# Gates and branches as [token, channel], with operand octets on multiples of 64 bytes

## The chip, the core and the metric

One core of a Trainium2 chip runs the whole program. Its engines work side by side and wait for each other through semaphores: TensorE (PE; its weight loads are shown apart as PEld), VectorE (DVE), ScalarE (ACT), GpSimd (POOL) and SyncE (SP), which here issues the loads. The metric is the device time of one execution in microseconds (us); lower is better.

## What is computed

Two decoder blocks over 256 tokens of 2048 channels, in float32. The change lies in the first block's mixer. Three branches (a gated delta rule, sliding-window attention, stick-breaking attention) give `y_dn` (1024 channels), `y_swa` and `y_sb` (512 each). Each is projected to 2048 channels, multiplied by a gate of its own, and the sum goes through one more projection:

```python
proj = xn @ w_in                       # gates: its last 3 * 2048 columns
gate = jax.nn.sigmoid(gates).reshape(bsz, seq, N_BRANCH, D_MODEL)
merged = gate[:, :, 0] * (y_dn @ w_br_dn) + gate[:, :, 1] * (y_swa @ w_br_swa) \
       + gate[:, :, 2] * (y_sb @ w_br_sb)
return merged @ w_o
```

`xn` is the RMS-normalized input. The rest (cross attention to `mem`, a gated MLP with a short convolution, and a second block with an HGRN recurrence, a pooling mixer and a squared-ReLU MLP) is as usual, and of it only the matmuls matter here.

## The kernel before

**Numbers.** A float32 matrix product is made of float32r products: each operand is split in a high part and a remainder, and three products are added (high x high, high x remainder, remainder x high). Weights come in *chunks* of 8 blocks of 128x128 (512 KB); SP loads two chunks at a time into `wr` (three such buffers). ACT writes a chunk's high part `wh` (`split_hi`, L264), DVE the remainder `wl` in two halves of 128x512 (`split_lo`, L273), two chunks ahead of their use. The program uses 854 chunks, and TensorE is meant to work on them without a pause.

**Operands.** Activations stand as [channel, token] in *octets*: tiles `[128, 8, 2, 256]` of float32r, 16 KB in each partition, that hold high part and remainder of 8 blocks of 128 channels. Two octets make an `Operand`. `P0` (P0a, P0b) and `P1` (P1a, P1b) live for the whole program, behind the tile of small vectors `vec`, which has 481 columns. In the built program they start at bytes 20512, 36896, 53280 and 69664 of each partition, all 32 past a multiple of 64. The octets P2a, P2b, P2c and YH, which some stages add, start on multiples of 64, and so do `wr`, `wh` and `wl`.

**Two forms of a product.** `gemm` calls `mm` (L283 to L291) for each block: the weights are stationary, and the octet's block moves, first high part and remainder together (512 columns, L290), then the high part again under the weights' remainder (256 columns, L291). The result is [channel, token], one block of 128 channels a bank, in two halves that `evac` (from L379) adds: ACT copies one, DVE adds the other and multiplies by the token's norm. `gemm_nat` (from L359) turns the roles: a block of the octet for 128 tokens is stationary, and 512 columns of weights move, in three matmuls (L373 high x high, L374 remainder x high, L375 high x remainder). The result is [token, channel], 512 channels in two banks, one for each half of the tokens. A chunk is 8 pairs in the first form and 12 matmuls in the second.

**Order.** All instructions are written out by one Python program in a fixed order. Beside the stream of matmuls run generators ("tasks") that emit their next instructions at a *slot*; there is one slot after each block of a chunk. `until` runs slots without matmuls until something holds.

**Around the change.** For each of 16 blocks of 128 channels, `gates(d)` makes three gates from `Ax` (the normalized input, in P0): 6 chunks, evacuated, multiplied by the norm, sigmoid. `branches(d, ...)` makes the three products from `Ay` (P1): 2 chunks, evacuated; POOL multiplies each by its gate and adds the three into `M[:, d]`. When the last `gates` is through, `merged_gen` splits the 16 blocks of `M` into `Am` (P0 again), from which the output projection `w_o` reads; it starts with two blocks of output side by side (`gemm_first`), so that the last 4 of the 16 input blocks are needed only after 24 pairs. During the 16 steps SP also loads `mem` and `x`, and ACT and POOL add up the squares of `mem` (`Sm`), whose column sums (L429) TensorE makes in the projection.

The second form is used before by five places: stick-breaking values (P0), cross-attention values (P0), values and gates of the second block (P1), and the last MLP's output (P0b, P2a, P2b, P2c in turn).

Of the kernel before, what the change touches and what calls it, by code (L numbers as in the profile page):

```python
# [9 lines left out]
F32 = mybir.dt.float32  # L10
# [3 lines left out]
AF = mybir.ActivationFunctionType  # L14
# [13 lines left out]
def _consts():  # L28
# [37 lines left out]
    ("ffn_conv", 192), ("norm_final", 16), ("norm_mix_pre_2", 16), ("norm_mix_post_2", 16),  # L66
    ("norm_mlp_pre_2", 16), ("pool_b_2", 8), ("pool_scale_2", 8),
    ("lb_logits_2", 16), ("hgrn_norm_w_2", 8), ("dn_norm", 1), ("dn_a_log", 8),
    ("dn_dt_bias", 8), ("swa_sinks", 8),
]  # L70
_VOFF = {}
_n = 0
for _k, _w in _VECS:
    _VOFF[_k] = (_n, _w)
    _n += _w
_VN = _n
FIRST = {"w_swa": 4, "w_o": 2, "w_mi": 4}


# [6 lines left out]
def tile_kernel(ctx, tc, a, out, dbg=None):  # L86
# [120 lines left out]
    plan("w_dn", 0, 64)  # L207
    plan("w_sbv", 0, 8)
    plan("w_sbqk", 0, 16)
    for d in range(16):  # L210
        plan("w_gate", 6 * d, 6)
        plan("w_br", 2 * d, 2)
    plan("w_o", 0, 32)
    plan("w_xq", 0, 8)
    plan("w_xk", 0, 8)
# [140 lines left out]
            if k == 15:  # L356
                then(t, ps[t])

    def gemm_nat(A):  # L359

        ps = []
        for c in range(8):
            w = Chunk()
            hv = w.h.rearrange("p (k n) c -> p k (n c)", k=2)
            lv = w.l.rearrange("p (k n) c -> p k (n c)", k=2)
            for t in range(2):
                if c == 0:
                    ps.append(bank("pn"))
                for k in range(2):
                    kk = 2 * c + k  # L370
                    wait_for(A, kk)
                    s, e = (c == 0 and k == 0), (c == 7 and k == 1)
                    PE.matmul(ps[t], A[kk][:, 0, cs(t)], hv[:, k], start=s, stop=False)  # L373
                    PE.matmul(ps[t], A[kk][:, 1, cs(t)], hv[:, k], start=False, stop=False)  # L374
                    PE.matmul(ps[t], A[kk][:, 0, cs(t)], lv[:, k], start=False, stop=e)  # L375
                    w.block(2)
        return ps
# [712 lines left out]
    def gate_gen(o, p):  # L1090
        yield from evac(o, p, Nx)
        act(o, o, AF.Sigmoid)
        yield 2
# [7 lines left out]
    def branch_gen(d, m, b, p, gate):
        o = M[:, d] if b == 0 else m[:, b - 1]
        yield from evac(o, p)
        G.tensor_tensor(o, o, gate, op=ALU.mult)
        if b == 2:
            yield 4
            G.tensor_tensor(m[:, 0], m[:, 0], m[:, 1], op=ALU.add)
            G.tensor_tensor(M[:, d], M[:, d], m[:, 0], op=ALU.add)
            yield 6
            merged[0] += 1  # L1110

    def branches(d, g3):
        m = mp.tile([128, 2, T], F32, name="m", tag="m", bufs=2)
        for b, (n0, n1) in enumerate(((0, 8), (8, 12), (12, 16))):
            p = bank()
            if b != 2:
                w = Chunk()
            for k in range(n0, n1):
                mm(p, w.h[:, k % 8], w.l[:, k % 8], Ay[k], k == n0, k == n1 - 1)
                w.block()  # L1120
            spawn(branch_gen(d, m, b, p, g3[:, b]))

    gp = gates(0)
# [5 lines left out]
    MT = mc.enter_context(tc.tile_pool(name="mt", bufs=1)).tile([128, 16, T], F32, name="MT")  # L1129
    mc2 = ExitStack()  # L1130
    mp = mc2.enter_context(tc.tile_pool(name="mm", bufs=1))
    M = mp.tile([128, 16, T], F32, name="M")
    Sm = Squares()
    Am = Operand(*P0)

    def merged_gen():
        for n in range(16):
            while merged[0] <= n:
                yield 1
            yield from split(Am, n, M[:, n])  # L1140

    for d in range(16):
        if d:
            gp = gates(d)
        if d == 15:
            spawn(merged_gen())
        branches(d, gp)
        if d < 8:
            s4 = slice(4 * (d % 4), 4 * (d % 4) + 4)
            nc.sync.dma_start(MT[:, s4] if d < 4 else X[:, s4], (a["mem"] if d < 4 else a["x"])[:, s4])  # L1150
        else:
            spawn(Sm.add(MT[:, 2 * d - 16]))
            spawn(Sm.add(MT[:, 2 * d - 15]), 4)

    def residual(n, p, gain, A, *sums):

# [532 lines left out]
            V.scalar_tensor_tensor(y, t, 1.5, y, op0=ALU.add, op1=ALU.mult)  # L1689
            return y  # L1690

    eps = cp.tile([128, 1], F32, name="eps")
    G.memset(eps, EPS)
    post5 = Post()
    S5 = post5.Sq
    gain5 = W("norm_mix_post_2")
# [55 lines left out]
    nat = {}  # L1752
    ss7 = ec.tile([128, 2, 4], F32, name="ss7")
    pre7 = ec.tile([128, 2], F32, name="pre7")

    def ch(g):
        return slice(512 * g, 512 * g + 512)

    def flip_x_gen():
        while not all(A2_.ok):  # L1760
# [151 lines left out]
def layout(i):  # L1912
    i = {k: np.asarray(v) for k, v in i.items()}
    cat = np.concatenate
    x = _feat(i["x"][0])
    o = {"x": x, "xg": cat([_vec(i["norm_mix"][0]), x[:, 0:2].reshape(128, -1)], 1), "mem": _feat(i["mem"][0]), "cst0": _CARR[0], "cst1": _CARR[1], "cst2": _CARR[2]}
    w = i["w_in"][0]
    qkv, z, ab, sq, skv, sb, gt = np.split(
        w, np.cumsum([3072, 1024, 16, 512, 256, 1536]), axis=1)
    grp = []  # L1920
    for g in range(4):
        s = slice(256 * g, 256 * g + 256)
        grp += [qkv[:, 1024:2048][:, s], qkv[:, 0:1024][:, s], qkv[:, 2048:][:, s], z[:, s]]
    o["w_dn"] = _tiles(cat(grp, 1))
    o["w_ab"] = ab.reshape(16, 128, 16).transpose(1, 0, 2).reshape(128, 256)
    sq = sq.reshape(D, 2, 4, 64).transpose(0, 2, 1, 3).reshape(D, 512)
    o["w_swa"] = _tiles(cat([skv, sq], 1))
    o["w_sbqk"] = _tiles(sb[:, 0:1024].reshape(D, 2, 4, 128).transpose(0, 2, 1, 3).reshape(D, 1024))
    o["w_sbv"] = _rows(sb[:, 1024:])
    o["w_gate"] = _tiles(gt.reshape(D, 3, 16, 128).transpose(0, 2, 1, 3).reshape(D, 6144))  # L1930
    swa = i["w_br_swa"][0].reshape(2, 4, 64, D).transpose(1, 0, 2, 3).reshape(512, D)
    o["w_br"] = _tiles(cat([i["w_br_dn"][0], swa, i["w_br_sb"][0]], 0))
# [40 lines left out]
    o["vec"] = cat([v[n] for n, _ in _VECS], 1)  # L1973
# [22 lines left out]
```

## Time and profile before

| | us |
|---|---|
| median of 3 runs (2615.05 to 2616.28) | 2615.83 |
| the profiled execution | 2615.93 |
| its span, first to last instruction | 2613.9 |
| TensorE busy in the span | 2572.2 |
| DVE busy | 1872.2 |
| ACT busy | 1363.3 |
| POOL busy | 341.0 |

The granted TensorE clock is 0.997 of full speed over the span. A matmul's row gives its start and how long it takes from start to end; since matmuls are pipelined, the next one starts earlier than that, and the distance of two starts is what it costs in a stream. In the rows by time the columns are start, duration, engine, line, operation, written tile <- read tiles, stationary and moving sizes; in brackets stands idle time ahead of it and what ended it.

### The profile page before, as it was taken

The page shows a single profiled execution, that of the slowest core. Times are in us where ns is not written, and L with a number is a line of the kernel's source. Part 1 is how long each engine was busy: PE and PEld are TensorE (multiplying, and loading weights), DVE is VectorE, ACT ScalarE, POOL GpSimd, SP SyncE. Part 2 cuts the span into 40 slices and gives each one's busy share as a digit, 9 for nine tenths or more (in the row PEclk, how much of TensorE's full clock was granted, in tenths as well). Part 3 has the DMA queues.
Part 4 walks back from the last instruction along what each step waited for, and adds up shares of the span by engine and source line. Part 5 has one row for each costly group of instructions (what it writes and reads, how often), then busy time and mean ns, then how long its engine had stood idle before and what let it go on. Part 6 is the DMA issues. An engine that isn't in the chain of part 4 may idle for free.

```text
span 2613.9 us, 39511 instructions
## 1 busy us (share of the span) xinstructions
PE 2572.2 (98%) x15277; PEld 2196.4 (84%) x15277; DVE 1872.2 (72%) x3487; ACT 1363.3 (52%) x2157; POOL 341.0 (13%) x326
## 2 busy tenths in 40 slices
PE   8999999999999999999999999999899999999998
PEld 7888888888888888888888888878788888888886
DVE  7787766667777788888866687976675575665665
ACT  6655545555555565555544454555564444443443
POOL 1122111222321010000001102721010000000000
PEclk9999999999999999999999999999999999999999
DMA  6433435555555445555555554345445555555553
GB/s 226 137 138 130 146 130 194 212 207 185 186 179 192 163 160 194 187 184 193 180 191 182 194 178 161 114 145 193 145 171 188 189 190 197 181 190 193 201 190 141
DMA packets 66428, 461.17 MB, mean 176 GB/s; under 512 B 7360, under 2 KB 7616, under 8 KB 11840
## 3 DMA queue, kind: packets, MB, share of 16 engines
q1 hardware_dynamic: 65952, 457.86, 50.2%
q8 instruction: 120, 1.97, 0.3%
q10 hardware_dynamic: 288, 0.79, 0.1%
q14 instruction: 68, 0.56, 0.1%
HBM read 456.52 MB, written 2.10 MB: 175 GB/s over the span
## 4 chain that ended last, share of the span: by engine, by line
PE 86%; DVE 8%; ACT 3%; issue 3%; POOL 0%; DVEq 0%; ACTq 0%; POOLq 0%
PE pg L290 40%; PE pg L291 20%; PE pn L373 6%; PE pn L374 6%; PE pn L375 6%; PE pg L288 3%; DVE wl L273 3%; PE pg L287 1%; ACT wh L264 1%; PE ph L1459 0%; PE pz L754 0%; DVE QK L987 0%; DVE Wt L1431 0%; DVE P0b L416 0%; DVE P1b L418 0%
## 5 line engine op out<-in xcount | busy, mean ns | idle before, releaser
L273 DVE TENSOR_TENSOR wl<-wr,wh 128x512 fp32r<-128x512 f32 x1708 | 1218.8, 749 | 308.6 <-ACT wh L264 307.6
L264 ACT ACTIVATE wh<-wr 128x1024 fp32r<-128x1024 f32 x854 | 902.9, 1058 | 860.8 <-PE pg L288 331.7
L290 PE MATMUL pg<-P1a,wh 128*128 128x512 f32 x1360 | 492.2, 400 | 4.6 <-DVE P1a L418 4.6
L290 PE MATMUL pg<-P1b,wh 128*128 128x512 f32 x1188 | 430.7, 399 | 1.4 <-ACT wh L264 1.4
L290 PE MATMUL pg<-P0a,wh 128*128 128x512 f32 x1040 | 383.0, 404 | 6.9 <-ACT wh L264 6.9
L291 PE MATMUL pg<-P1a,wl 128*128 128x256 f32 x1360 | 383.5, 282 | 3.3 <-DVE wl L273 3.3
L290 PE MATMUL pg<-P0b,wh 128*128 128x512 f32 x1031 | 378.6, 403 | 0.3 <-DVE P0b L416 0.3
L291 PE MATMUL pg<-P1b,wl 128*128 128x256 f32 x1188 | 334.7, 282 | 2.9 <-DVE wl L273 2.8
L290 PEld LDWEIGHTS pg<-P1a,wh 128*128 128x128 f32 x1360 | 257.0, 189 | 59.0 <-issue 5.0
L291 PE MATMUL pg<-P0a,wl 128*128 128x256 f32 x1040 | 292.9, 282 | 0.0
L291 PE MATMUL pg<-P0b,wl 128*128 128x256 f32 x1031 | 289.9, 281 | 1.1 <-DVE wl L273 1.1
L291 PEld LDWEIGHTS pg<-P1a,wl 128*128 128x128 f32 x1360 | 258.4, 190 | 13.6 <-DVE wl L273 6.1
L290 PEld LDWEIGHTS pg<-P1b,wh 128*128 128x128 f32 x1188 | 223.3, 188 | 53.9 <-ACT wh L264 2.0
L290 PEld LDWEIGHTS pg<-P0a,wh 128*128 128x128 f32 x1040 | 196.6, 189 | 48.3 <-ACT wh L264 6.8
L290 PEld LDWEIGHTS pg<-P0b,wh 128*128 128x128 f32 x1031 | 193.7, 188 | 46.7 <-issue 1.2
L291 PEld LDWEIGHTS pg<-P1b,wl 128*128 128x128 f32 x1188 | 224.6, 189 | 6.9 <-DVE wl L273 5.1
L291 PEld LDWEIGHTS pg<-P0a,wl 128*128 128x128 f32 x1040 | 197.5, 190 | 6.5 <-DVE wl L273 0.7
L291 PEld LDWEIGHTS pg<-P0b,wl 128*128 128x128 f32 x1031 | 194.7, 189 | 2.1 <-DVE wl L273 1.6
L492 POOL TENSOR_TENSOR Sq<-Sq,q 128x512 f32<-128x512 f32 x48 | 70.3, 1464 | 459.3 <-ACT q L484 459.1
L383 DVE TENSOR_TENSOR t<-t,pg 128x256 f32<-128x256 f32 x79 | 33.0, 421 | 91.0 <-ACT t L381 91.0
L1291 POOL TENSOR_TENSOR cv<-cv 128x256 f32<-128x256 f32 x32 | 33.1, 1034 | 327.4 <-DVE cv L1285 327.4
L288 PE MATMUL pg<-P1b,wh 128*128 128x512 f32 x188 | 75.0, 399 | 0.0
(566 smaller groups left out, 3873.2 us busy)
## 6 DMA issues: line engine op xcount, KB each, us to landing
wr<-in_w_up_dram SPq DMA_DIRECT2D x64, 1024.0 KB, 4.9
wr<-in_w_mi_dram SPq DMA_DIRECT2D x64, 1024.0 KB, 4.9
wr<-in_w_mo_dram SPq DMA_DIRECT2D x64, 1024.0 KB, 4.9
wr<-in_w_gate_dram SPq DMA_DIRECT2D x48, 1024.0 KB, 4.9
wr<-in_w_dn_dram SPq DMA_DIRECT2D x32, 1024.0 KB, 4.9
wr<-in_w_down_dram SPq DMA_DIRECT2D x32, 1024.0 KB, 4.9
wr<-in_w_br_dram SPq DMA_DIRECT2D x16, 1024.0 KB, 4.9
wr<-in_w_o_dram SPq DMA_DIRECT2D x16, 1024.0 KB, 4.9
```

The lines of the kernel that those rows point to most:

```text
L264: S.activation(h, r, AF.Copy)
L273: V.tensor_sub(l[:, s], r[:, s], h[:, s].bitcast(F32))
L287: PE.matmul(o[:, T:2 * T], l, A[:, 0], start=False, stop=False)
L288: PE.matmul(o, h, both, start=False, stop=True)
L290: PE.matmul(o, h, both, start=start, stop=False)
L291: PE.matmul(o[:, T:2 * T], l, A[:, 0], start=False, stop=False)
L373: PE.matmul(ps[t], A[kk][:, 0, cs(t)], hv[:, k], start=s, stop=False)
L374: PE.matmul(ps[t], A[kk][:, 1, cs(t)], hv[:, k], start=False, stop=False)
L375: PE.matmul(ps[t], A[kk][:, 0, cs(t)], lv[:, k], start=False, stop=e)
L383: V.tensor_add(dst, dst, p[:, 0:T])
L492: G.tensor_tensor(self.S, self.S, q, op=ALU.add)
L1291: G.tensor_tensor(cv[:, 0], cv[:, 0], cv[:, 1], op=ALU.mult)
```

## The change

**Alignment.** `vec` is padded to a multiple of 16 columns (it gets one more, `eps`, a constant that a memset wrote before, and is 496 columns wide). In the built program P0a, P0b, P1a and P1b then start at 20544, 36928, 53312 and 69696, multiples of 64. All other large tiles keep their places.

**Form.** The 12 gate products (3 gates, 4 groups of 512 channels) are made by `gemm_nat` on `Ax`, 8 chunks each, and the 12 branch products by `gemm_nat` on `Ay`, 4, 2 and 2 chunks. Weights are laid out for it on the host. A gate is one sigmoid per token half, read from the bank, with the token's norm as the activation's scale. A branch is, per token half, one multiplication by the gate out of the bank on DVE and, for the second and third branch, one addition into `M`, which is now [token, channel]. Both have 128x512 elements. POOL has no part in it.

**Order.** Four steps of 24 gate chunks and 8 branch chunks replace sixteen of 6 and 2. One gate product (8 chunks) instead of three (6 chunks) stands ahead of the point where the tasks of the mixers are drained. The loads of `mem` and `x` and the squares of `mem` are spread over the products, and the squares end ahead of the last step's branches. `merged_gen` transposes the sum: 8 groups of 4 transposes of 128x128 on TensorE (L1134), each split from its bank into two blocks of `Am`; it begins with the last step's branches.

On TensorE, the first branch after the gates (`pg` and `pn` are the banks, P1a the octet, `wh` and `wl` the weights). Before:

```order
L287 MATMUL pg<-P0b,wl 128x256
L288 MATMUL pg<-P0b,wh 128x512
L290 MATMUL pg<-P1a,wh 128x512 [waits Activation_49]
L291 MATMUL pg<-P1a,wl 128x256 [waits DVE_49]
L290 MATMUL pg<-P1a,wh 128x512
L291 MATMUL pg<-P1a,wl 128x256
```

Now:

```order
L374 MATMUL pn<-wh,P0b 128x512
L375 MATMUL pn<-wl,P0b 128x512
L373 MATMUL pn<-wh,P1a 128x512 [waits Activation_49]
L374 MATMUL pn<-wh,P1a 128x512
L375 MATMUL pn<-wl,P1a 128x512 [waits DVE_49]
L373 MATMUL pn<-wh,P1a 128x512
```

Each pair of 512 and 256 columns has become part of a triple of 512 columns.

On TensorE in the output projection: before, the column sums of mem's squares, which wait for POOL, after 19 pairs.

```order
L290 MATMUL pg<-P0b,wh 128x512 [waits DVE_49]
L291 MATMUL pg<-P0b,wl 128x256
L429 MATMUL pr<-cst_72,Sq 128x1 [waits Pool_49]
L429 MATMUL pr<-cst_72,Sq 128x1
L290 MATMUL pg<-P0b,wh 128x512
```

Now, after 6 pairs, the seventh group of transposes, which waits for DVE:

```order
L290 MATMUL pg<-P0a,wh 128x512
L291 MATMUL pg<-P0a,wl 128x256
L1134 MATMUL px<-cst_72,M 128x128 [waits DVE_49,PE_49]
L1134 MATMUL px<-cst_72,M 128x128 [waits DVE_49]
L1134 MATMUL px<-cst_72,M 128x128 x2
L290 MATMUL pg<-P0a,wh 128x512
```

The column sums now follow 5 pairs behind it, and one pair later comes the eighth group.

On DVE at the end of the last step's branches, now (L1119 multiplies by the gate, L1122 adds into `M`, L273 makes the weights' remainders):

```order
L273 TENSOR_TENSOR wl<-wr,wh 128x512 [waits PE_49,Activation_49]
L273 TENSOR_TENSOR wl<-wr,wh 128x512
L1119 TENSOR_TENSOR g_4829<-pn,g_4829 128x512 [waits PE_49]
L1122 TENSOR_TENSOR M<-M,g_4829 128x512 [waits DVE_49]
L1119 TENSOR_TENSOR g_4830<-pn,g_4830 128x512 [waits PE_49]
L1122 TENSOR_TENSOR M<-M,g_4830 128x512 [waits DVE_49]
L273 TENSOR_TENSOR wl<-wr,wh 128x512 [waits DMAHW2_49,Activation_49]
```

The four operations that the seventh group needs stand behind one chunk's two remainders and ahead of the next chunk's.

The diff, cut to its core:

```diff
-    ("dn_dt_bias", 8), ("swa_sinks", 8),
+    ("dn_dt_bias", 8), ("swa_sinks", 8), ("eps", 1),
...
-_VN = _n
+_VN = -(-_n // 16) * 16
...
-    for d in range(16):
-        plan("w_gate", 6 * d, 6)
-        plan("w_br", 2 * d, 2)
+    for d in range(4):
+        plan("w_gate", 24 * d, 24)
+        plan("w_br", 8 * d, 8)
...
-    def gemm_nat(A):
+    def gemm_nat(A, cs_=range(8)):
...
-    def gates(d):
-        g3 = tp.tile([128, 3, T], F32, name="g3", tag="g3")
-        for b in range(3):
-            spawn(gate_gen(g3[:, b], gemm(Ax)))
-        return g3
...
+    def gate_gen(o, ps):
+        for t in range(2):
+            act(o[t], ps[t], AF.Sigmoid, scale=Nx.rc[:, t:t + 1])
+            free(ps[t])
+            yield 2
...
-    M = mp.tile([128, 16, T], F32, name="M")
+    M = mp.tile([128, 2, D], F32, name="M")
...
+    def branch_gen(d, b, ps, g):
+        for t in range(2):
+            m = M[:, t, ch(d)]
+            V.tensor_tensor(g[t] if b else m, ps[t], g[t], op=ALU.mult)
+            free(ps[t])
+            if b:
+                V.tensor_tensor(m, m, g[t], op=ALU.add)
+            yield 2
+        merged[0] += 1
...
     def merged_gen():
-        for n in range(16):
-            while merged[0] <= n:
+        for j in range(8):
+            while merged[0] < 3 * (j // 2 + 1):
                 yield 1
-            yield from split(Am, n, M[:, n])
...
+            ps = pss.tile([128, 2, T], F32, name="px", tag="s")
+            for i in range(2):
+                for t in range(2):
+                    PE.transpose(ps[:, i, cs(t)], M[:, t, cs(2 * j + i)], ident)
+            yield 2
+            yield from split(Am, slice(2 * j, 2 * j + 2), ps)
+            yield 2
...
+    side = beside()
+    for d in range(4):
+        g = []
+        for b in range(3):
...
+                g.append(gate(last[b]))
+            next(side, None)
+        last = g
+        if d == 3:
+            spawn(merged_gen())
+        for b, (c0, c1) in enumerate(((0, 4), (4, 6), (6, 8))):
+            spawn(branch_gen(d, b, gemm_nat(Ay, range(c0, c1)), g[b]))
+            next(side, None)
...
-    eps = cp.tile([128, 1], F32, name="eps")
-    G.memset(eps, EPS)
+    eps = W("eps")
```

`beside` issues, one at a time between the products, the eight loads of `mem` and `x` and then the squares of `mem`.

More of the change, by code (lines that the diff above doesn't have):

```diff
@@ L357, in gemm_first @@
                 then(t, ps[t])
-    def gemm_nat(A):
+    def gemm_nat(A, cs_=range(8)):
         ps = []
-        for c in range(8):
+        for c in cs_:
             w = Chunk()
@@ L366, in gemm_nat @@
             for t in range(2):
-                if c == 0:
+                if c == cs_[0]:
                     ps.append(bank("pn"))
@@ L371, in gemm_nat @@
                     wait_for(A, kk)
-                    s, e = (c == 0 and k == 0), (c == 7 and k == 1)
+                    s, e = (c == cs_[0] and k == 0), (c == cs_[-1] and k == 1)
                     PE.matmul(ps[t], A[kk][:, 0, cs(t)], hv[:, k], start=s, stop=False)
@@ L1088, in tile_kernel, with ch, gate @@
     merged = [0]
[L1090 to L1093, printed above, removed]
-    def gates(d):
-        g3 = tp.tile([128, 3, T], F32, name="g3", tag="g3")
-        for b in range(3):
-            spawn(gate_gen(g3[:, b], gemm(Ax)))
-        return g3
[L1101 to L1123, printed above, removed]
+    def ch(g):
+        return slice(512 * g, 512 * g + 512)
+    def gate_gen(o, ps):
[3 more added lines that the diff above has]
+            yield 2
+    def gate(o):
+        spawn(gate_gen(o, gemm_nat(Ax)))
+        return o
+    g0 = gate([tp.tile([128, 512], F32, name="g3", tag="g3") for _ in range(2)])
     drain()
@@ L1136, in merged_gen @@
     def merged_gen():
-        for n in range(16):
-            while merged[0] <= n:
+        for j in range(8):
+            while merged[0] < 3 * (j // 2 + 1):
                 yield 1
-            yield from split(Am, n, M[:, n])
[L1142 to L1145, printed above, removed]
-            spawn(merged_gen())
[L1147 to L1153, printed above, removed]
+            ps = pss.tile([128, 2, T], F32, name="px", tag="s")
[5 more added lines that the diff above has]
+            yield 2
@@ new lines, in beside @@
+    def beside():
+        for to, name in ((MT, "mem"), (X, "x")):
+            for q in range(4):
+                nc.sync.dma_start(to[:, 4 * q:4 * q + 4], a[name][:, 4 * q:4 * q + 4])
+                yield
+        for _ in range(4):
+            yield
+        for n in range(0, 16, 2):
+            spawn(Sm.add(MT[:, n]))
+            spawn(Sm.add(MT[:, n + 1]), 4)
+            yield
+    side = beside()
+    for d in range(4):
+        g = []
+        for b in range(3):
+            if d == 0 and b == 0:
+                g.append(g0)
+                continue
+            if d == 0 or d == 1 and b == 0:
+                g.append(gate([mp.tile([128, 512], F32, name=f"g{b}{t}") for t in range(2)]))
+            else:
+                g.append(gate(last[b]))
+            next(side, None)
+        last = g
+        if d == 3:
+            spawn(merged_gen())
+        for b, (c0, c1) in enumerate(((0, 4), (4, 6), (6, 8))):
+            spawn(branch_gen(d, b, gemm_nat(Ay, range(c0, c1)), g[b]))
+            next(side, None)
@@ L1155, in residual @@
+    for _ in side:
+        pass
     def residual(n, p, gain, A, *sums):
@@ L1754, in tile_kernel @@
     pre7 = ec.tile([128, 2], F32, name="pre7")
-    def ch(g):
-        return slice(512 * g, 512 * g + 512)
     def flip_x_gen():
@@ L1929, in layout @@
     o["w_sbv"] = _rows(sb[:, 1024:])
-    o["w_gate"] = _tiles(gt.reshape(D, 3, 16, 128).transpose(0, 2, 1, 3).reshape(D, 6144))
+    o["w_gate"] = cat([_rows(gt[:, 2048 * b + 512 * d:][:, :512]) for d in range(4) for b in range(3)], 0)
     swa = i["w_br_swa"][0].reshape(2, 4, 64, D).transpose(1, 0, 2, 3).reshape(512, D)
-    o["w_br"] = _tiles(cat([i["w_br_dn"][0], swa, i["w_br_sb"][0]], 0))
+    w = cat([i["w_br_dn"][0], swa, i["w_br_sb"][0]], 0)
+    o["w_br"] = cat([_rows(w[:, 512 * d:][:, :512]) for d in range(4)], 0)
     o["w_o"] = _tiles(i["w_o"][0])
@@ L1972, in layout @@
         v[n] = np.broadcast_to(i[n][0][None], (128, 8))
-    o["vec"] = cat([v[n] for n, _ in _VECS], 1)
+    v["eps"] = np.full((128, 1), EPS, np.float32)
+    o["vec"] = np.pad(cat([v[n] for n, _ in _VECS], 1), ((0, 0), (0, _VN - _n)))
     for k, x in o.items():
```

## The prediction

> **What bounds the kernel now.** I read the page's first and fourth part, then windows, then the order of time at four places.
>
> ```profile
> span 2613.9 us, 39511 instructions
> PE 2572.2 (98%) x15277; PEld 2196.4 (84%) x15277; DVE 1872.2 (72%) x3487; ACT 1363.3 (52%) x2157; POOL 341.0 (13%) x326
> ...
> PE 86%; DVE 8%; ACT 3%; issue 3%; POOL 0%; DVEq 0%; ACTq 0%; POOLq 0%
> ```
>
> TensorE is the bound: 98% busy, 86% of the chain that ended last. What the change does to DVE, ACT or POOL counts only where TensorE has to wait for it. But "busy" of a pipelined engine hides its pace, so I take starts, not durations.
>
> The windows view of the gates and branches, and the order of time at three points of it (first branch matmul of the first and of the last of the 16 steps, and the first matmul of the output projection):
>
> ```profile
> 395.60:757.00 361.40, 361.40 (x2056) 314.63 (x2056) 250.66 (x405) 193.12 (x299) 88.00 (x82) 1.00 0.56 197
> ...
> 412.55 0.40 PE L290 MATMUL pg<-P1a,wh 128*128 128x512 f32 x1
> ...
> 751.35 0.40 PE L290 MATMUL pg<-P1a,wh 128*128 128x512 f32 x1
> ...
> 756.99 0.40 PE L290 MATMUL pg<-P0a,wh 128*128 128x512 f32 x1
> ```
>
> TensorE never stops here: 361.40 of 361.40 us, clock 1.00. DVE works 250.66 us, ACT 193.12 us, the DMA engines 0.56 of the time. 15 steps take 751.35 - 412.55 = 338.8 us, so one step of 8 chunks of weights takes 22.59 us, a chunk 2.823 us, and each of its 8 pairs (512 + 256 columns) 352.9 ns. The whole stage is 16 x 22.59 = 361.4 us.
>
> **The change, part by part.**
>
> *The new form of the matmuls (128 chunks).* A chunk becomes 12 matmuls of 512 columns with the octet as the stationary operand: 12 x 512 columns, as many as 8 x 768. So columns save nothing; the overhead per matmul decides, and the kernel has that form already in the last MLP and four other places. There are octets there on both kinds of address: P2a to P2c lie on multiples of 64 bytes, P0 and P1 are 32 bytes off. The starts of the triples in the order of time (first and last of stretches without anything between):
>
> ```profile
> 1556.76 0.39 PE L373 MATMUL pn<-wh,P1b 128*128 128x512 f32 x1
> ...
> 1561.66 0.40 PE L373 MATMUL pn<-wh,P1b 128*128 128x512 f32 x1
> ...
> 2001.51 0.39 PE L373 MATMUL pn<-wh,P0b 128*128 128x512 f32 x1
> ...
> 2004.78 0.39 PE L375 MATMUL pn<-wl,P0b 128*128 128x512 f32 x1
> ...
> 2167.79 0.39 PE L374 MATMUL pn<-wh,P2b 128*128 128x512 f32 x1
> ...
> 2173.91 0.39 PE L374 MATMUL pn<-wh,P2c 128*128 128x512 f32 x1
> ```
>
> Off the multiple, 21 starts on P1b take 4.90 us and 14 on P0b 3.27 us: 233.3 and 233.6 ns each, say 233.5. On it, 27 starts take 6.12 us: 226.7 ns each. A chunk of gates thus takes 12 x 226.7 = 2.720 us in place of 2.823, and the stage 128 x 2.720 = 348.2 us: **-13.2 us**. Without the alignment it would be 12 x 233.5 = 2.802 us and only -2.7 us.
>
> The Trainium skill, "TensorE: Matmul & The Clock Gate", section "Back-to-back issue gap", has N/2.4 + 2.5 ns per matmul: 215.8 ns for 512 columns, 109.2 for 256. By that a chunk would take 2.600 us as pairs and 2.590 as triples, and this term would be an estimated -1.3 us. The trace disagrees on both forms (352.9 ns a pair against 325, 226.7 against 215.8).
>
> *The same alignment where that form was used before.*
>
> ```profile
> L373 PE MATMUL pn<-wh,P0b 128*128 128x512 f32 x160 | 63.6, 398 | 0.0
> ...
> L373 PE MATMUL pn<-wh,P1a 128*128 128x512 f32 x64 | 26.6, 415 | 0.0
> L373 PE MATMUL pn<-wh,P1b 128*128 128x512 f32 x64 | 26.1, 407 | 0.0
> L373 PE MATMUL pn<-wh,P0a 128*128 128x512 f32 x32 | 13.2, 411 | 0.0
> ```
>
> Each row stands for three lines (L373 to L375), so 576 matmuls on P0 and 384 on P1 get 6.8 ns shorter: 3.9 and 2.6 us. P0's are in stages where TensorE waits for nothing. P1's are the values and gates of the second block, and beside and behind them TensorE waits for the recurrence's own chain:
>
> ```profile
> PE pg L291 <- DVE wl L273: 3.2, 6, 1.0
> PE ph L1534 <- DVE ho L1529: 2.1, 2, 1.3
> PE ph L1475 <- POOL pq L1467: 1.5, 1, 1.5
> ```
>
> Work that ends sooner in front of such a wait lengthens the wait. I take half: **-5.2 us**, bounds -3.9 and -6.5.
>
> *Aligned octets as the moving operand.* That is the rest of the program: about 3930 pairs on P0 and P1 outside the gates (4950 by the counts of L290 and L288, less 1024). Here the trace answers too, since the first MLP's down projection reads P0 and P2 in turn, 16 pairs each:
>
> ```profile
> 1378.08 0.39 PE L290 MATMUL pg<-P2a,wh 128*128 128x512 f32 x1
> ...
> 1383.72 0.39 PE L290 MATMUL pg<-P0a,wh 128*128 128x512 f32 x1
> ...
> 1389.36 0.39 PE L290 MATMUL pg<-P2a,wh 128*128 128x512 f32 x1
> ```
>
> 5.64 us with aligned octets, 5.64 with misaligned ones: **0**. The rows' 0.01 us over 16 pairs leaves 0.6 ns a pair open, 2.5 us either way.
>
> *Transposes.* The sum must be turned back, 8 groups of 4 transposes. The second block has such groups between pairs:
>
> ```profile
> 1904.16 0.28 PE L291 MATMUL pg<-P1b,wl 128*128 128x256 f32 x1
> 1904.28 0.60 PE L1767 MATMUL px<-cst,X 128*128 128x128 f32 x4
> 1904.63 0.48 PE L290 MATMUL pg<-P1b,wh 128*128 128x512 f32 x1
> 1904.95 0.28 PE L291 MATMUL pg<-P1b,wl 128*128 128x256 f32 x1
> ```
>
> From 1904.28 to 1904.95 is 0.67 us where the matmul alone takes 0.235: 0.435 us a group, **+3.5 us**.
>
> *The seam to the output projection.* Before, TensorE waits there twice:
>
> ```profile
> 763.76 0.28 PE L291 MATMUL pg<-P0b,wl 128*128 128x256 f32 x1
> 765.15 0.61 PE L429 MATMUL pr<-cst,Sq 128*128 128x1 f32 x4 [1.10 <-POOL Sq L494]
> ...
> 768.44 0.28 PE L291 MATMUL pg<-P0b,wl 128*128 128x256 f32 x1
> 769.04 0.50 PE L290 MATMUL pg<-P0b,wh 128*128 128x512 f32 x1 [0.32 <-DVE P0b L416]
> ```
>
> 1.39 us less a matmul's 0.12, and 0.60 less 0.12: 1.8 us in all. Both go: POOL no longer multiplies the gates, the squares of mem are all added before the last branches, and three quarters of the sum are split before the seam. Late next are the transposes of the last 512 channels, 6 pairs (2.1 us) into the projection; 18 pairs are queued behind them on TensorE before the first that reads their result. They need the last branch's four DVE operations of 128x512. The nearest row for those is the residual of the weights:
>
> ```profile
> 755.34 0.69 DVE L273 TENSOR_TENSOR wl<-wr,wh 128x512 fp32r<-128x512 f32 x1
> ```
>
> 4 x 0.69 = 2.76 us. The first half can start when the first token half's bank is complete, 7 starts (1.6 us) ahead of the seam, plus the 0.39 us that a matmul takes to end; but two residuals of weights stand ahead of it on DVE, until some 0.3 us ahead of the seam. That ends near 2.5 us against 2.1: a wait of some 0.5 us, bounds 0 (DVE free in time) and 2.3 (one more pair of residuals in front). So **-1.3 us**, bounds -1.8 and +0.5.
>
> *At nothing.* The sigmoid now reads PSUM in 128x512 on ACT, with the token's norm as its scale; 24 of them and the 40 DVE operations of the branches replace 288 of 128x256 on ACT and DVE and 80 on POOL, and the sum's split is 16 of 128x512 in place of 32. They lie under TensorE (193 of 361 us ACT, 251 DVE before); price without that cover in the rivals. On SP's queue the eight loads of mem and x move between the weight loads, 0.5 MB each beside about 1 MB per 5.44 us at the densest, 1.4 times the window's 197 GB/s at 0.56 busy, so 0.8 or so. The longer vec (60 bytes) and eps from it: one load at the start, one memset less.
>
> **Sum.** -13.2 - 5.2 + 0 + 3.5 - 1.3 = -16.2 us. The profiled execution took 2615.93 us (span 2613.9 and 2.0 around it), the median is 2615.83, so the base is the same to 0.1: **2599.6 us**. All bounds at their best give -13.2 - 6.5 - 2.5 + 3.5 - 1.8 = -20.5 (2595.4), at their worst -13.2 - 3.9 + 2.5 + 3.5 + 0.5 = -10.6 (2605.3).
>
> **Rivals.**
>
> 1. *The 6.8 ns are of the place, not of the offset.* P0 and P1 lie low in the memory, P2 high, and the change moves nothing far. Then the gates run at 233.5 ns (-2.7), the old uses gain nothing: -2.7 + 3.5 - 1.3 = -0.5, **2615.4 us**. For: every slow octet is low, every fast one high, so the trace cannot part the two. Against: P0b and P1b, 32 KB apart, share one pace to 0.3 ns, and the run from P2b into P2c has the other throughout; a matter of place should show steps between. The Trainium skill speaks for this rival: "SBUF — State Buffer", section "Specifications (TRN2)", has cachelines of 16 bytes, and an operand 32 bytes past a multiple of 64 starts on such a line already, so the shift would be worth nothing; no run here shows the line's size. Chance 0.13.
>
> 2. *DVE falls behind at the short branches.* Two of the three branches of a step have 2 chunks, 5.44 us of TensorE. DVE has in each 4 residuals and up to 4 operations of the branch before. At 0.69 that is 5.5 us, just even; at the stage's mean of 812 ns for a residual it is 6.0:
>
> ```profile
> L273 DVE TENSOR_TENSOR wl<-wr,wh 128x512 fp32r<-128x512 f32 x254 | 196.2, 812 | 18.2 <-ACT wh L264 18.1
> ```
>
> 0.56 us late, 8 times, is 4.5 us: -11.7, **2604 us**. For: DVE works in order, and an operation on the last matmul's bank holds the residuals behind it. Against: the 812 were beside POOL's multiplications, which go; and residuals run two chunks ahead. Chance 0.13.
>
> 3. *The pairs get slower on aligned octets, and the kernel with them.* The first MLP shows equal means, but its aligned runs are 16 pairs between misaligned ones. If in long runs the pairs stay in the slower of the spacings seen there (1378.78 to 1379.13 is short, 1379.48 to 1379.84 long, 0.36):
>
> ```profile
> 1378.78 0.40 PE L290 MATMUL pg<-P2a,wh 128*128 128x512 f32 x1
> ...
> 1379.13 0.40 PE L290 MATMUL pg<-P2a,wh 128*128 128x512 f32 x1
> ...
> 1379.48 0.40 PE L290 MATMUL pg<-P2a,wh 128*128 128x512 f32 x1
> ...
> 1379.84 0.40 PE L290 MATMUL pg<-P2a,wh 128*128 128x512 f32 x1
> ```
>
> that is 7 ns more on 3930 pairs, +27.5 us: **2627 us**, slower. It decides from 4.1 ns a pair on (16.2 / 3930). Against: the spacings alternate within a run, and the sum over 16 pairs is equal. Chance 0.06.
>
> **How the numbers follow.** Forecast 0.68, rivals 0.13, 0.13 and 0.06. The forecast's own range is 2595.4 to 2605.3. To hold 8 in 10 I take in the second rival: 4.5 us on the forecast's worst is 2609.8, and I stop at 2609; below, 2594 leaves 1.4 us for waits that vanish unseen. Outside lie the first and third. A measurement of this kernel tells about 0.2% (5.2 us) from no change: faster than 2610.6 is the forecast and rival 2, 0.81; the same is rival 1, 0.13; slower is rival 3, 0.06.
>
> **What would show it.** In the changed profile: starts of L373 to L375 on P0 and P1 226.7 ns apart (233.5: rival 1); 16 pairs of L290 on P0 still 5.64 us; the stage from the first gate matmul to the projection about 348 us and 2.6 us of transposes (6 of the 8 groups), TensorE without gaps (gaps on L375 that end with DVE: rival 2); no wait of L429 there, and one of at most 0.5 us at the seventh group of transposes. The prediction is wrong if the pace of the gates is not 226.7, or if the stages behind the projection change by more than the 5 us of the old uses.

## The result and the profile after

The changed kernel takes 2601.33 us (median of 4 runs, 2599.39 to 2601.73), the kernel before, on the same chip, 2615.44 us (4 runs, 2614.77 to 2616.28). The ratio is 0.9944 with a 95% interval of 0.9927 to 0.9962: faster by 14 us, where 16.2 were predicted. The time lies in the predicted range. The reason that the prediction gave for most of it does not hold, though: it is not the multiple of 64 bytes that an octet lies on. The experiments below show what it is instead.

The page of the changed kernel, its first lines:

```profile
span 2599.9 us, 38275 instructions
PE 2558.5 (98%) x14797; PEld 2172.4 (84%) x14797; DVE 1811.5 (70%) x3375; ACT 1327.3 (51%) x2027; POOL 254.3 (10%) x245
```

TensorE is still the bound, at 98% of a span that is 14.0 us shorter. DVE lost 61 us of work, ACT 36, POOL 87, and none of that shows in the time by itself.

The windows view of the gates and branches (busy time of PE, PEld, DVE, ACT, POOL; clock; DMA share; GB/s):

```profile
395.30:746.00 350.70, 350.70 (x1569) 290.56 (x1568) 196.53 (x302) 160.18 (x180) 11.44 (x9) 1.00 0.58 203
```

TensorE has no gap here. DVE is busy for 196.5 us instead of 250.7.

In the order of time, the first and the last of 48 matmuls of the new form without anything between, on P0b in the gates and on P2b in the last MLP:

```profile
428.37 0.39 PE L373 MATMUL pn<-wh,P0b 128*128 128x512 f32 x1
...
439.02 0.39 PE L375 MATMUL pn<-wl,P0b 128*128 128x512 f32 x1
...
2145.32 0.40 PE L373 MATMUL pn<-wh,P2b 128*128 128x512 f32 x1
...
2155.98 0.39 PE L375 MATMUL pn<-wl,P2b 128*128 128x512 f32 x1
```

47 starts in 10.65 and 10.66 us: 226.6 and 226.8 ns each. The predicted pace is there, on P0 and on P2.

The seam to the output projection, TensorE and DVE in the order of time:

```profile
746.38 0.68 DVE L1119 TENSOR_TENSOR g<-pn,g 128x512 f32<-128x512 f32 x1
747.10 0.69 DVE L1122 TENSOR_TENSOR M<-M,g 128x512 f32<-128x512 f32 x1
747.71 0.68 DVE L1119 TENSOR_TENSOR g<-pn,g 128x512 f32<-128x512 f32 x1
748.43 0.69 DVE L1122 TENSOR_TENSOR M<-M,g 128x512 f32<-128x512 f32 x1
748.76 0.28 PE L291 MATMUL pg<-P0a,wl 128*128 128x256 f32 x1
748.88 0.84 PE L1134 MATMUL px<-cst,M 128*128 128x128 f32 x4
749.48 0.48 PE L290 MATMUL pg<-P0a,wh 128*128 128x512 f32 x1
...
751.21 0.28 PE L291 MATMUL pg<-P0a,wl 128*128 128x256 f32 x1
751.32 0.50 PE L429 MATMUL pr<-cst,Sq 128*128 128x1 f32 x4
```

The seventh group of transposes occupies TensorE from 748.88 to 749.48, 0.60 us. The groups inside the last branches take 0.35, so it waits 0.25 us, for the last addition of DVE, which ends at 749.12. L429 follows the pair ahead of it with its usual 0.11 us: that wait is gone.

Stage by stage, the two traces differ as follows. A stage's time is the distance of the starts of two splits on ACT, of its third chunk and of the next stage's third; the splits run two chunks ahead of TensorE.

| us | predicted | measured |
|---|---|---|
| gates and branches, with 6 groups of transposes (-13.2 + 2.6) | -10.6 | -10.9 |
| output projection, with 2 groups and the seam (+0.9 - 1.3) | -0.4 | -0.6 |
| P0's old uses: two value projections -0.44, -0.50; last MLP, two quarters of -1.28 | -3.9 | -3.5 |
| second block's values to gates (P1's old uses): -0.99, +1.58, -0.54 | -1.3 | +0.1 |
| stages of pairs behind the projection | 0 ± 2.5 | +1.0 |

### The profile page after: what moved, and what is told of

It is laid out like the page before. It is cut to its first block, busy times and chain, and to the rows that moved or that the text cites. A ratio compares the mean times of both kernels' runs of the same rounds, so it can differ in the third digit from the quotient of the medians.

```text
span 2599.9 us, 38275 instructions
## 1 busy us (share of the span) xinstructions
PE 2558.5 (98%) x14797; PEld 2172.4 (84%) x14797; DVE 1811.5 (70%) x3375; ACT 1327.3 (51%) x2027; POOL 254.3 (10%) x245
## 4 chain that ended last, share of the span: by engine, by line
PE 60%; DVE 4%; ACT 2%; issue 1%; POOL 0%; DVEq 0%; ACTq 0%; POOLq 0%
PE pg L290 25%; PE pg L291 13%; PE pn L373 6%; PE pn L375 6%; PE pn L374 6%; DVE wl L273 2%; PE pg L288 2%; PE pg L287 1%; ACT wh L264 1%; PE ph L1477 1%; DVE P1b L418 0%; ACT hj L1541 0%; DVE P1a L418 0%; DVE M L1742 0%; POOL Wt L1455 0%
## 5 line engine op out<-in xcount | busy, mean ns | idle before, releaser
L273 DVE TENSOR_TENSOR wl<-wr,wh 128x512 fp32r<-128x512 f32 x1708 | 1187.9, 731 | 436.9 <-ACT wh L264 436.0
L290 PE MATMUL pg<-P1b,wh 128*128 128x512 f32 x1092 | 396.3, 401 | 1.4 <-ACT wh L264 1.4
L290 PE MATMUL pg<-P0b,wh 128*128 128x512 f32 x695 | 257.2, 406 | 0.0
L290 PE MATMUL pg<-P0a,wh 128*128 128x512 f32 x656 | 245.1, 409 | 7.4 <-ACT wh L264 7.4
L291 PE MATMUL pg<-P0b,wl 128*128 128x256 f32 x695 | 195.1, 281 | 1.1 <-DVE wl L273 1.1
L291 PE MATMUL pg<-P0a,wl 128*128 128x256 f32 x656 | 185.0, 282 | 0.0
L290 PEld LDWEIGHTS pg<-P0a,wh 128*128 128x128 f32 x656 | 124.4, 190 | 33.5 <-ACT wh L264 7.4
L373 PE MATMUL pn<-wh,P0b 128*128 128x512 f32 x352 | 137.5, 391 | 0.0
L375 PE MATMUL pn<-wl,P0b 128*128 128x512 f32 x352 | 137.0, 389 | 0.0
L374 PE MATMUL pn<-wh,P0b 128*128 128x512 f32 x352 | 137.0, 389 | 0.0
L291 PEld LDWEIGHTS pg<-P0b,wl 128*128 128x128 f32 x695 | 131.3, 189 | 1.9 <-DVE wl L273 1.4
L291 PEld LDWEIGHTS pg<-P0a,wl 128*128 128x128 f32 x656 | 125.0, 191 | 4.2 <-DVE wl L273 0.7
```

Source lines behind the costliest of these rows:

```text
L273: V.tensor_sub(l[:, s], r[:, s], h[:, s].bitcast(F32))
L290: PE.matmul(o, h, both, start=start, stop=False)
L291: PE.matmul(o[:, T:2 * T], l, A[:, 0], start=False, stop=False)
```

## The experiments

### The alignment alone

```diff
-    ("dn_dt_bias", 8), ("swa_sinks", 8),
+    ("dn_dt_bias", 8), ("swa_sinks", 8), ("eps", 1),
-_VN = _n
+_VN = -(-_n // 16) * 16
-    eps = cp.tile([128, 1], F32, name="eps")
-    G.memset(eps, EPS)
+    eps = W("eps")
```

The kernel before, with the change's part on `vec` and `eps` only; gates and branches keep their form.

> The kernel before with the four octets of P0 and P1 on multiples of 64 bytes (vec padded, eps in it) and nothing else. Theory (a stationary operand off the multiple costs each 512-column matmul about 6.8 ns; as a moving operand the octet's address is free): L373 to L375 on P0 and P1 start 226.7 ns apart; the stages with P0 lose 576 x 6.8 = 3.9 us, those of the second block (P1) nothing, because the waits beside them take up the 2.6 us; 2615.4 - 3.9 = 2611.5 us. By the prediction's half for P1: 2610.2. Rival (the pace is of the place in the memory, low or high): 233.5 ns as before, 2615.4. Rival (the gain of the whole change comes from the form): 2615.4.

Measured: 2611.32 us (2610.86 to 2613.41), ratio 0.9984 (0.9975 to 0.9994). In the order of time of this kernel, 48 matmuls on P0b in the values of the cross attention:

```profile
912.42 0.39 PE L373 MATMUL pn<-wh,P0b 128*128 128x512 f32 x1
...
923.08 0.40 PE L375 MATMUL pn<-wl,P0b 128*128 128x512 f32 x1
```

226.8 ns. So the shift of P0 and P1 by 32 bytes does bring their triples to the faster pace, and rival 1, by which it would bring nothing, falls. The stages on P0 change by -0.45, -0.50, -1.28 and -1.28 us.

### The form alone

```diff
-    eps = W("eps")
+    eps = cp.tile([128, 1], F32, name="eps")
+    G.memset(eps, EPS)
-_VN = -(-_n // 16) * 16
+_VN = _n
```

The changed kernel with P0 and P1 back where they were (32 bytes lower).

> The changed kernel with P0 and P1 back at 32 bytes past a multiple of 64 (vec not padded, eps in its own tile); all other tiles where they were. Theory: all 1536 + 960 matmuls of the second form on P0 and P1 start 233.5 ns apart; against the changed kernel the gates and branches lose 10.4 us and the stages with P0 3.9 us, the others nothing: 2601.3 + 14.3 = 2615.6, as the kernel before: the form alone is worth nothing, since the transposes (3.5 us) cost what its pace (2.7) and the seam (1.3) give. Rival (the place, or the form alone): 2601 to 2602.

Measured: 2613.41 us (2612.57 to 2614.1), ratio 0.9992 (0.9982 to 1.0001). Its 48 matmuls on P0b in the gates:

```profile
428.23 0.40 PE L373 MATMUL pn<-wh,P0b 128*128 128x512 f32 x1
...
439.20 0.39 PE L375 MATMUL pn<-wl,P0b 128*128 128x512 f32 x1
```

233.4 ns. Gates and branches gain 1.2 us, the projection 0.7. No gain was expected (2615.6 us); the run is 2.4 us below the kernel before, though the interval of the ratio just takes in 1. By the stages the form alone is worth about 2 us and the shift in P0's old uses 3.5. Most of the 14 us needs both, since it is the faster pace of the 1536 new matmuls: from this run to the changed kernel the gates and branches fall from 363.70 to 353.95 us, 9.7 us (1536 x 6.7 ns would be 10.3). Together that is 15 us, of which the stages of pairs behind the projection take back 1.0.

### Octets on other offsets

```diff
+OFF = {'P0b': 4, 'P1a': 8, 'P1b': 12, 'P2b': 8}
...
-        return pool.tile([128, 8, 2, T], F32R, name=name, tag=tag or name)
+        f = OFF.get(name)
+        if f is None:
+            return pool.tile([128, 8, 2, T], F32R, name=name, tag=tag or name)
+        t = pool.tile([128, 16 * T + 16], F32R, name=name, tag=tag or name)
+        return t[:, f:f + 16 * T].rearrange("p (k a t) -> p k a t", a=2, t=T)
```

(`OFF` counts elements of 4 bytes.)

> The changed kernel with offsets from a multiple of 64 bytes of 16 for P0b, 32 for P1a, 48 for P1b, and 32 for P2b, which lies high in the memory; P0a, P2a and P2c stay on the multiple. Theory (64 bytes decide, wherever the octet lies): 226.7 ns between starts on P0a, P2a, P2c and 233.5 on P0b, P1a, P1b and P2b alike. Rival (lines of 16 bytes): 226.7 on all. Rival (32 bytes decide): 226.7 on P1a and P2b too, 233.5 on P0b and P1b. Rival (place): P2b stays at 226.7.

Measured: 2606.08 us in one run. It broke the theory. P0a still lay on a multiple of 64 bytes, and its 48 matmuls were slow:

```profile
418.38 0.40 PE L378 MATMUL pn<-wh,P0a 128*128 128x512 f32 x1
...
429.35 0.39 PE L380 MATMUL pn<-wl,P0a 128*128 128x512 f32 x1
```

233.4 ns; P1b, on no such multiple, went at 228.3. And the pairs on P1, whose pace no alignment had changed so far, got faster: the first MLP's wide product took 354.67 us instead of 359.02. The padding of the octets had also moved them against the weight tiles.

### All large tiles shifted together

```diff
-_VN = _n
+_VN = -(-_n // 16) * 16
-    o["vec"] = cat([v[n] for n, _ in _VECS], 1)
+    o["vec"] = np.pad(cat([v[n] for n, _ in _VECS], 1), ((0, 0), (0, _VN - _n)))
```

The kernel before with the padding alone: `eps` stays a tile of its own, and with it wr, wh, wl, P2 and YH now start 32 bytes past a multiple of 64, while P0 and P1 start on one. Against before, everything behind `vec` has moved by 32 bytes, and no distance between an octet and a weight tile has changed.

> The kernel before with vec padded but eps left in its own tile of 32 bytes: P0 and P1 come to multiples of 64, while all that lies behind them (wr, wh, wl, P2a to P2c, YH) moves 32 bytes off. Theory (the stationary operand's address decides): the second form takes 226.7 ns on P0 and P1 and 233.5 on P2; in the first form wh and wl are the stationary operands, so its pairs get up to 2 x 6.8 = 13.6 ns longer, 366 instead of 353, on all 5330 pairs: up to 72 us, 2690; if their pace is set by something other than the weight load, 353 and 2618. Rival (the moving operand's address decides): the second form slows on all octets, since wh and wl move there, and the first form does not change.

Measured: 2615.89 us in one run, as the kernel before. 48 matmuls on P0b and on P2b:

```profile
912.74 0.40 PE L373 MATMUL pn<-wh,P0b 128*128 128x512 f32 x1
...
923.71 0.39 PE L375 MATMUL pn<-wl,P0b 128*128 128x512 f32 x1
...
2158.11 0.40 PE L373 MATMUL pn<-wh,P2b 128*128 128x512 f32 x1
...
2168.77 0.39 PE L375 MATMUL pn<-wl,P2b 128*128 128x512 f32 x1
```

P0b, now on a multiple of 64, is slow (233.4 ns); P2b, now off it, is fast (226.8 ns). So the octet's own address is not what counts. What fits all runs up to here is the distance from the weight tile to the octet modulo 256 bytes. Before, wh starts at byte 110656 and P0a at 20512: -90144, or 224 modulo 256, while P2 and YH are at 0. The change moved P0 and P1 by 32 bytes and left wh in place, so all octets came to 0. (256 is what the addresses bear out: with the change P0a's distance, -90112, is a multiple of 512 too, and P2a's, 169280 - 110656 = 58624, is 256 past one, and both go at 226.7 ns; at a distance of 128 it is 232.4, as the table below shows.)

### Other distances

Two kernels with the octets at other distances, by a padding and an offset for each:

```diff
+OFF = {'P0a': (4, 16), 'P0b': (8, 16), 'P1a': (0, 16), 'P1b': (0, 16), 'P2a': (12, 64), 'P2b': (28, 64), 'P2c': (36, 64)}
...
-        return pool.tile([128, 8, 2, T], F32R, name=name, tag=tag or name)
+        f, n = OFF.get(name, (0, 0))
+        t = pool.tile([128, 16 * T + n], F32R, name=name, tag=tag or name)
+        return t[:, f:f + 16 * T].rearrange("p (k a t) -> p k a t", a=2, t=T)
```

The second has the same edit with `P0a (12, 16), P0b (12, 16), P1a (12, 16), P1b (4, 16), P2a (36, 64), P2b (40, 64), P2c (60, 64)`.

> The changed kernel with the octets at other distances, modulo 256 bytes, from the weights' high part: P0a 16, P0b 96, P1a 128, P1b 192, P2a 48, P2b 112, P2c 144. New theory (the distance between stationary and moving operand decides, modulo 256; the addresses' own remainder does not): the second form takes 226.7 ns a matmul at 0, some 228 at 16, and 232 to 233.5 at the others. Rival (modulo 128): 226.7 at P1a. Rival (multiples of 64 for each operand): 226.7 at P1a and P1b, 233.5 at the rest. For the first form the pairs were 353 ns at 0 and at 224 and 347 at 160: by the theory of distances they have a curve of their own, so P1a, P1b and P0b lie between 346 and 354; by the rival that only the octet's remainder counts, P1a and P1b stay at 353.

> As the run beside it, with distances P0a 48, P0b 112, P1a 176, P1b 208, P2a 144, P2b 160, P2c 240. Theory of distances: in the second form the same octet names change their pace with the distance and not with the name: P2a 233 here (144), P2c 228 here (240), all others 232 to 233.5; in the first form P1a (176) about 347 as at 160, P1b (208) on the way to 353. Rival (place or name): P2a, P2b, P2c keep what they have in the run beside it.

Measured: 2614.81 and 2611.25 us, one run each. A third kernel filled gaps with distances that are 8 past a multiple of 16 (`P0a (2, 8), P0b (2, 8), P1a (26, 32), P1b (14, 16), P2a (38, 64), P2b (6, 64), P2c (14, 64)`):

> The changed kernel with the octets at distances P0a 8, P0b 40, P1a 168, P1b 248, P2a 152, P2b 24, P2c 56 bytes from the weight tile, modulo 256, to fill the two curves (ns a triple matmul, ns a pair). From the neighbours so far: triples 226.7 to 232 at 8 and 248 (between 0 and 16, and 240 and 0), 233.3 at all others; pairs 347 to 349 at 40, 56, 152 and 168, 350 to 353 at 8, 24 and 248. Looked for: a distance that is fast for both forms, 8 or 248 if there is one. The time is a mixture, about 2610 us.

Measured: 2626.74 us in one run, slower than the kernel before. The paces in all these traces, by the distance of the octet from the weight tile: ns from start to start of a triple's matmuls (mean over the triples that another on the same octet follows), and ns a pair in the first form (the same, on P1 and P2). Both leave out those with a wait of TensorE.

| distance, bytes mod 256 | a triple's matmul | a pair |
|---|---|---|
| 0 | 226.7 | 352.0 to 353.3 (348.9 in one run) |
| 24 | 231.3 | 358.0 |
| 32 | 233.3 | 348.8 |
| 48 | 233.3 | 346.4 and 347.6 |
| 112 | 233.3 | 352.5 |
| 128 | 232.4 | 350.6 |
| 144 | 233.3 | 347.6 |
| 152 | 231.1 | 354.7 |
| 160 | 233.3 | 346.9 to 348.5 |
| 168 | 233.3 | 354.9 |
| 176 | 230.0 | 349.6 |
| 192 | 229.0 | 352.5 |
| 208 | 232.5 | 352.3 |
| 224 | 233.3 | 352.2 to 353.6 |
| 240 | 228.3 | 350.0 |
| 248 | 233.3 | 358.8 |

For triples, 0 is the best place. On P0 and P2c there are seven more distances for them: 230.7 ns at 8, 232.2 at 16, 233.3 at 40 and 56, 233.4 at 64, 231.9 at 80, 234.3 at 96; so everywhere else they lose 1.6 to 7.6 ns on average. For pairs 48, 144 and 160 are best, and the four distances of the table that are 8 past a multiple of 16 are worst (P0b at 40, another such distance, has 349 to 354 ns by stage and doesn't fit). What the third kernel looked for, a distance next to 0 that is fast in both forms, is not at 248.

Of the rivals, the two by other multiples fall with P1a, which has 232.4 ns at 128, and the one by name with P2c, which has 233.3 at 144 and 228.3 at 240. But the curve was forecast badly: 176, 192, 24 and 152 are faster for triples than expected, 248 is slower, the pairs at 24, 152, 168 and 248 were all put too low, and the third kernel's 2610 us became 2626.74.

Nor does the distance decide alone everywhere. Two stretches of 48 matmuls on P0a at 16, both in the gates of the first of the three kernels:

```profile
439.43 0.40 PE L376 MATMUL pn<-wh,P0a 128*128 128x512 f32 x1
...
450.40 0.39 PE L378 MATMUL pn<-wl,P0a 128*128 128x512 f32 x1
...
484.01 0.39 PE L376 MATMUL pn<-wh,P0a 128*128 128x512 f32 x1
...
494.66 0.39 PE L378 MATMUL pn<-wl,P0a 128*128 128x512 f32 x1
```

The first goes at 233.4 ns, the second at 226.6: one octet, one distance, two paces, and the 232.2 above is their mixture. Pairs differ likewise. In the first MLP's down projection of that kernel the first 8 pairs on P0a take 346.8 ns each and the later ones 360.0, and P2a at 0 has 348.9 in the run with octets on other offsets, where its neighbour P2b lay at 32. What plays in besides the distance was not tried.

### Only the weight tiles moved

The sharpest test of the distance: `wh` and `wl` start 32 bytes later, while P0 and P1 stay where the change put them. P2 and YH, which lie behind the weights, come 256 bytes later by the second gap, so that their place modulo 256 stays too.

```diff
+        if i == 0:
+            wp.tile([128, 8], F32, name="gap", tag="gap", bufs=1)
         h = wp.tile([128, 8, 128], F32R, name="wh", tag="wh", bufs=3)
         l = wp.tile([128, 8, 128], F32R, name="wl", tag="wl", bufs=3)
+        if i == 2:
+            wp.tile([128, 56], F32, name="gap2", tag="gap2", bufs=1)
```

> The changed kernel with one difference: the weight tiles wh and wl begin 32 bytes later; every octet stays where the change put it, on a multiple of 256 bytes. Theory now (what counts is the distance from the weight tile to the octet, modulo 256 bytes): it is 224 for all octets, P2 and YH too, so all triples go at 233.3 ns, P2's in the last MLP too, which were at 226.7 in every run so far in which P2 kept distance 0. Gates and branches +10.1 us, P0's old uses +3.8, the last MLP's 1536 matmuls +10.2, P1's old uses about 0 (the recurrence waits there): about 2624 us, slower than the kernel before. If an octet's own multiple of 64 bytes counted after all: 226.7 and 2601 us.

(The expectation speaks of multiples of 256 bytes. The octets lie on multiples of 64: 20544 is 64 past a multiple of 256. The argument rests on the distances alone.)

Measured: 2622.19 us in one run, 21 above the changed kernel. 48 matmuls on P0b in the gates, and on P2b in the last MLP:

```profile
429.72 0.40 PE L377 MATMUL pn<-wh,P0b 128*128 128x512 f32 x1
...
440.69 0.39 PE L379 MATMUL pn<-wl,P0b 128*128 128x512 f32 x1
...
2158.50 0.39 PE L377 MATMUL pn<-wh,P2b 128*128 128x512 f32 x1
...
2169.47 0.39 PE L379 MATMUL pn<-wl,P2b 128*128 128x512 f32 x1
```

Both at 233.4 ns, P2b for the first time, although all octets lie on multiples of 64. Gates and branches take 9.7 us longer, P0's value projections 0.45 and 0.49, the four quarters of the last MLP's output 10.1 together. (The expectation counted P0b's 384 matmuls in that MLP twice, 2.6 us; without that it is about 2622.)

### Each octet at the distance of its own use

P1 serves the two wide stages of pairs; P0 and P2 serve mostly triples. So P1a goes to 48 and P1b to 160, and the others stay at 0.

```diff
+OFF = {'P1a': (12, 16), 'P1b': (24, 48)}
```

with the tile function of the kernels of other distances.

> The changed kernel with P1a 48 and P1b 160 bytes from the weight tile modulo 256 in place of 0; P0, P2 and YH stay at 0. In the runs with other distances the pairs went at 347 ns a pair at 48 and 160 and at 352 to 353 at 0; the triples at 233.3 at both and 226.7 at 0. Theory (distance decides, for each form its own): the two wide stages of pairs on P1, 2 x 128 chunks of 8 pairs, get 5.2 to 6 ns a pair shorter, -11 to -12 us; the 32 chunks of branches lose 384 x 6.6 ns = 2.5 us; the few triples elsewhere on P1 lie beside the recurrence's waits: about 0, at most -1 with its shorter waits. About 2591.5 us (2589 to 2594), 0.9905 of the kernel before, 10 us below the changed one. If pairs and triples both only followed the multiple of 64: slower than the changed kernel.

Measured: 2592.9 us (2591.59 to 2594.49), ratio 0.9909 to the kernel before (0.9893 to 0.9926), 8.4 us below the changed kernel's median, which was taken on another chip. Windows of the first MLP's wide product and of one quarter of the last MLP's input product, the changed kernel first:

```profile
945.28:1304.31 359.03, 358.76 (x2029) 310.61 (x2029) 294.38 (x546) 202.91 (x323) 34.46 (x33) 1.00 0.54 188
2054.90:2145.57 90.67, 90.67 (x515) 78.61 (x514) 62.61 (x124) 45.09 (x64) 0.00 (x0) 1.00 0.53 186
```

and this one:

```profile
947.99:1301.49 353.50, 353.22 (x2029) 309.02 (x2029) 294.17 (x546) 201.82 (x322) 34.41 (x33) 1.00 0.55 191
2052.11:2141.30 89.19, 89.19 (x515) 78.22 (x514) 62.52 (x124) 45.11 (x65) 0.00 (x0) 1.00 0.55 189
```

The same instructions, 5.5 and 1.5 us less: 5.4 ns a pair in the first (1024 pairs), 5.8 in the second (256). The branches pay 2.4 us of it back, as expected. This version beats both kernels, by an edit that only moves two tiles.

## Why the prediction was right, and where it was not

**The gates' pace.** 226.7 ns forecast and found, and the stage's sum with it. The number was right because the change does set what decides; the reason given, the multiple of 64 bytes, was wrong. To that extent the forecast was lucky: the same 32 bytes that bring P0 and P1 to a multiple of 64 also bring them to distance 0. The trace of before could not part the two: in it, all fast octets were at distance 0 and on multiples of 64, all slow ones at 224 and off them.

**Rival 1, the place.** Fallen with the alignment alone. Its step closest to the truth was that the offset of the octet by itself need not matter. The cachelines of 16 bytes in the Trainium skill ("SBUF — State Buffer", "Specifications (TRN2)") don't tell which shift pays: the shift by 32 bytes was worth 6.7 ns a matmul where it changed the distance, and nothing where all tiles moved together.

**P0's old uses.** -3.9 forecast, -3.5 found.

**P1's old uses.** The mis-sized term: -1.3 forecast as half of 2.6, +0.1 found. The prediction looked for the loss in longer waits for the recurrence. What came was a lower clock behind such a wait. Windows about it, the changed kernel (the column ahead of the last two is the granted clock):

```profile
1605.17:1608.17 3.00, 2.55 (x15) 1.98 (x14) 3.00 (x6) 1.34 (x2) 2.65 (x3) 1.00 0.86 322
1608.17:1610.17 2.00, 0.87 (x8) 0.87 (x8) 2.00 (x3) 0.53 (x1) 1.08 (x1) 0.97 0.03 12
1610.17:1616.17 6.00, 6.00 (x23) 5.42 (x24) 4.98 (x10) 1.89 (x4) 3.92 (x4) 0.50 0.00 0
```

the kernel before:

```profile
1619.17:1622.17 3.00, 1.51 (x10) 1.08 (x8) 3.00 (x4) 0.96 (x1) 2.78 (x3) 1.00 0.60 251
1622.17:1624.17 2.00, 2.00 (x14) 1.86 (x15) 1.77 (x5) 1.26 (x2) 1.11 (x2) 0.82 0.02 4
1624.17:1626.17 2.00, 2.00 (x10) 1.90 (x10) 1.94 (x4) 0.00 (x0) 2.00 (x2) 0.50 0.00 0
```

and the alignment alone:

```profile
1618.17:1620.17 2.00, 0.42 (x4) 0.33 (x4) 2.00 (x3) 0.00 (x0) 1.61 (x2) 1.00 0.37 156
1620.17:1627.17 7.00, 7.00 (x52) 6.52 (x52) 6.77 (x12) 3.22 (x5) 5.20 (x6) 1.00 0.09 13
```

TensorE pauses for about 1.5 us in each of the three. Then the clock stays at half for a while in the changed kernel, for half as long before, and not at all with the alignment alone. Summed over windows of 1 us from 1500 to 1700, the time lost to it is 3.42, 1.70 and 0 us, and in every other run one of these three values. From the second block's values to its gates the three took 175.03, 174.98 and 173.76 us.

These three differ in the clock as well as in the pace, so they don't price the pace. Runs with the same clock do. With 3.42 us lost, the kernel with all large tiles shifted together and the one with P1 at 48 and 160 (P1's triples at 233.3 to 233.5 ns in both) took 176.16 us each; the changed kernel, at 226.7, took 175.03. So the faster triples were worth 1.1 us, near the forecast of 1.3. The clock took that back: at the slow pace the stages took 176.16 us with 3.42 us lost and 174.90 to 174.99 with 1.70 (the kernel before, the form alone, the weight tiles moved), 1.2 us less. What the prediction missed is the clock, which it does not mention; its half of 2.6 us was nearly right.

What decides between none, one and two such stretches was not tried. The Trainium skill, "TensorE: Matmul & The Clock Gate", section "Part 1: The HAM clock gate (the "warmup" mystery)", has a clock that is either full or half, and windows of 3413 ns that run freely; half of one or two such windows is 1.71 and 3.41 us, and the trace agrees. It puts the fall after an idle window of about 3.4 us; here the clock fell behind pauses of 1.4 to 1.6 us with eight matmuls of one column after them.

**Transposes and seam.** The groups inside the branches take four rows in 0.35 us and delay the next matmul by 0.09: 0.44 us, as forecast. The seventh group waits 0.25 us, where 0.5 was forecast within 0 to 2.3.

**DVE at the short branches (rival 2).** Fallen: TensorE has no gap in the stage. The groups of DVE in that window of the changed kernel:

```profile
L273 DVE TENSOR_TENSOR wl<-wr,wh 128x512 fp32r<-128x512 f32 x255 | 168.5, 701 | 148.5 <-ACT wh L264 148.5
L1122 DVE TENSOR_TENSOR M<-M,g 128x512 f32<-128x512 f32 x14 | 10.3, 737 | 0.5
L1119 DVE TENSOR_TENSOR g<-pn,g 128x512 f32<-128x512 f32 x14 | 9.6, 683 | 0.0
```

A residual of the weights takes 701 ns on average where it took 812, as the prediction held against this rival. The traces point to POOL: a residual that overlaps no instruction of POOL takes 686 ns before and 688 now, one that does took 1036 ns before; there were 90 of those then, and there are 7 now. The operations of the branches cost about as much as a residual, the row that they were priced by.

**Pairs on shifted octets (rival 3).** Fallen as forecast for this shift: from 224 to 0 the pairs' pace changes by less than 1 ns (0.16 us in a quarter with 256 pairs of the last MLP, 0.6 ns a pair). But pairs do depend on the distance, by 12 ns between 160 and 248. With P1 at 168 and 248 the rival's mechanism is there: the third kernel of the distances lost 4.3 us in the first MLP's wide product alone.

## What to carry to other kernels

Where a stream of matmuls runs without gaps and yet not at one pace, compare the addresses of the stationary and the moving operand with each other, modulo 256 bytes, before looking at either alone; a few bytes of padding ahead of a tile were worth 0.3% of this kernel (8.4 us) and, ahead of the weight tiles, cost 0.8% (21 us). In the kernel before, the width of an unrelated small tile had put P0 and P1 at their slow distance. One offset is not best for all forms: sort the operands by the form that uses them most. And where a trace offers a rule, look for what else is equal in its examples: two properties that always went together were told apart by moving all tiles at once, and then the weights alone. Trust such a curve only at the places that were measured: between them the forecasts often missed.

## What was not expected of the hardware

- The spacing of matmuls in a gapless stream depends on the distance between the operands' addresses: with 512 columns and new weights each time 226.7 ns at 0 modulo 256 bytes, 228.3 to 234.3 on average elsewhere; for a pair of 512 and 256 columns 346 to 360 ns, with another best distance. At 16 one octet had two paces, 226.6 and 233.4 ns, so the distance is not all. What costs the time, and whether wh or wl matters more, stays open: the two moved together in all runs.
- Behind a pause of TensorE of about 1.5 us, with eight matmuls of one column after it, the clock was at half for 3.4 us in seven of the eleven traces, for 6.8 us in three, and in one not at all.
- The shift of all large tiles by 32 bytes, at equal distances, changed no stage between the first 12 chunks and the recurrence by more than 0.16 us.
